# Conformer convolution: layout change of the product tiles by SBUF-to-SBUF transfers, and a provisional mean in half 0's layer norm

## The chip, the cores and the metric

The kernel runs on one core of a Trainium2 chip. The metric is the device time of one execution in microseconds (us). A change of under 0.2% (4.9 us) counts as no change here.

Five engines work side by side, each through its own list of instructions in order: TensorE (PE in the rows; PEld are its weight loads), VectorE (DVE), ScalarE (ACT), GpSimd (POOL) and SyncE (SP), which here only issues transfers. An instruction that waits holds up everything behind it in its engine's list. A transfer issued by ScalarE stands in ScalarE's list in the same way.

## The reference, cut to what matters

The program computes two layers over 1024 latent tokens with 1024 channels. The change is in the second layer's mixer, the Conformer convolution module:

```
u = xm @ w1 + b1;  a, g = split(u);  v = a * sigmoid(g)
v = depthwise conv along the tokens (31 taps) of v, + b
v = silu(layernorm(v))          # over the 1024 channels of a token
h = h + g1 * (v @ w2 + b2)
```

A feed-forward block and a final norm follow, which the change leaves alone.

## The kernel before

Channels lie on the 128 partitions and tokens on the free axis, so the 1024 channels are eight tiles m = 0 to 7, and the 1024 tokens are two halves of 512. Matrix products are made in three passes from a value split in a high and a low part (`whi`, `wlo` for weights, `xmh`, `xml` or `cxh`, `cxl` for data).

For each tile m, `conformer` does the following. TensorE makes the gate's product (`col_tile` into PSUM tile 0) and the value's (into tile 1). ScalarE takes the sigmoid into the tile `vt` (in the trace: `raw`), and VectorE multiplies in line 1253 or, in `taps`, line 1238. Then the depthwise convolution is made in one of two ways:

- Tiles 0, 2, 4 and 6 (`TAPS`): VectorE adds 30 shifted copies, one instruction each (line 1245, in the rows `CV<-ps,vec,CV`, some 1.3 us apart).
- Tiles 1, 3, 5 and 7 (`PRODS`): TensorE makes it as 108 small products (`conv`). For this the tile has to change its layout: tokens are grouped by their number modulo 4 (phases), and 32 channels times 4 phases must lie on the 128 partitions. The kernel writes the tile to DRAM (`vdr`) and reads it back rearranged into `xr` (also a `raw` buffer) with four transfers. ScalarE and VectorE split `xr` into `cxh` and `cxl`. After the products, VectorE copies PSUM tile 3 out to `yt` in two halves, and `yt` goes by way of DRAM (`cdr`) back to channel order in `yr` (in the rows: `sC`), from which ScalarE adds the bias into `CV`.

`conv(1)` follows tile 2's products, `conv(3)` those of tile 4, and `conv(5)` and `conv(7)` both follow tile 7's. Each needs five weight slots: four of eight steps, and a last one of four. Each slot is loaded by SyncE into one of two `wraw` buffers, copied to `whi` by ScalarE, and subtracted to `wlo` by GpSimd or VectorE in turns. A step is three products of 256 columns.

After that, half 0's layer norm (`center` with `sums`): the sum of the eight tiles is made from a running sum `lna[0]` (tiles 0 to 4) and the tiles 5, 6 and 7 (`LATE`) by products with an all-ones matrix; VectorE subtracts the mean from the eight tiles; ScalarE squares them; eight more products with ones give the variance; ScalarE takes the root and VectorE the reciprocal. Then the tiles are scaled, passed through silu, split (`xmh`, `xml`), and multiplied with w2 (`k_outer`).

The order of instructions on each engine is set by a planner in the program (`Order`): each operation has an estimated duration, a priority (`prio`, lower first) and buffers that it reads and writes, and the planner hands out the operation that it believes can start first. TensorE's order is the order in which the code calls it. A transfer costs SyncE `max(0.1, bytes / 340e3)` us in this plan and lands 2.0 us later; one on ScalarE costs 0.08 us. These are the plan's numbers, not the chip's. The program gives the transfers eight completion semaphores in turn: a transfer waits until the one that had its semaphore before has landed.

Of the kernel before, what the change touches and what calls it, by code (L numbers as in the profile page):

```python
# [21 lines left out]
ND = D // P  # L22
# [258 lines left out]
class Net:  # L281
    def __init__(self, nc, tc, es, a, out):
        self.nc, self.tc, self.a, self.out = nc, tc, a, out
        self.o = Order()
        self.mm_us = 0.2165
        pp = es.enter_context(tc.tile_pool(name="persist", bufs=1))
        ps = es.enter_context(tc.tile_pool(name="psum", bufs=1, space=bass.MemoryType.PSUM))
        dr = es.enter_context(tc.tile_pool(name="dram", bufs=1, space=bass.MemoryType.DRAM))
        self.P = [ps.tile([P, 2, 512], F32, name=f"ps{i}") for i in range(4)]
        self.PB = [[Buf(), Buf()] for _ in range(4)]  # L290
        self.vec = pp.tile([P, _NV], F32, name="vec")
        self.vB = Buf(True)
# [12 lines left out]
        self.ttall = pp.tile([P, 3 * 512], F32, name="tt")
        self.tt = Ring([(self.ttall[:, i * 512:i * 512 + 512], Buf()) for i in range(3)])
        self.acc = [(pp.tile([P, 512], F32, name=f"nacc{h}"), Buf()) for h in range(2)]
        self.rs = (pp.tile([P, 512], F32, name="rs"), Buf())
        self.mod = [pp.tile([P, 48], F32, name=f"mod{l}") for l in range(2)]
        self.modB = [[Buf() for _ in range(6)] for _ in range(2)]  # L310
        self.A = [pp.tile([P, 8], F32, name=f"A{n}") for n in range(5)]
        self.AB = [Buf(True) for _ in range(5)]
        self.gb = pp.tile([P, 8], F32, name="gb")
        self.gbB = Buf(True)
        self.eps = pp.tile([P, 1], F32, name="eps")
        self.epsB = Buf(True)
        self.sp8 = pp.tile([P, 2 * NR], F32, name="sp8")
        self.nsp8 = pp.tile([P, 2 * NR], F32, name="nsp8")
        self.nsp16 = pp.tile([P, 2 * NR], F32, name="nsp16")
        self.spB = Buf(True)  # L320
        self.cs = pp.tile([P, 16], F32, name="cs")
        self.modc = pp.tile([P, 16], F32, name="modc")
        self.cA = pp.tile([P, 8], F32, name="cA")
        self.ydr = dr.tile([NR, P, 1024], F32, name="ydr")
        self.ydrB = [[Buf(), Buf()] for _ in range(NR)]
        self.vdr = dr.tile([ND, P, 1024], F32, name="vdr")
        self.cdr = dr.tile([ND, P, 1024], F32, name="cdr")
        self.wq = []
        self.wq_load = self.wq_split = self.wq_use = 0
        self.wloaded, self.wsplit = {}, {}  # L330
# [862 lines left out]
    def conformer(self, pool):  # L1193
        nc, o = self.nc, self.o
        W, HS = 1024, 4
        CV = pool.tile([P, ND, W], F32, name="CV")
# [16 lines left out]
        phases = lambda t: t.rearrange("p (s i) -> p i s", i=4)  # L1213
        split = lambda t: t.rearrange("p (i s) -> p i s", i=4)
        flat = lambda pt: self.P[pt].rearrange("p a b -> p (a b)")
        inB = [Buf() for _ in range(ND)]
        outB = [[Buf(), Buf()] for _ in range(ND)]

        def sigmoid(m, pt):
            if m in TAPS:  # L1220
# [27 lines left out]
        def glu(m, pt):  # L1248

            if m in TAPS:  # L1250
                taps(m, pt)
                return
            self.stt(W, split(vt), phases(flat(pt)), self.v("cf_b_pw1", m), split(vt), ADD, MULT, self.PB[pt] + [vB], [vB], prio=-3)
            self.dma(self.vdr[m], vt, P * W * 4, r=[vB], w=[inB[m]], prio=-2)
            src = self.vdr[m].rearrange("(j c) (i s) -> i c j s", j=4, i=4)
            xrB.begin()
            for i in range(4):
                self.dma(split(xr)[32 * i:32 * i + 32], src[i], 131072, r=[inB[m]], wp=[xrB], prio=-2)
            hi, lo, hB, lB = xs[m // 2 % 2]
            inner = lambda t: t[:, :, HS:HS + 256]  # L1260
            self.act(W, inner(hi), split(xr), AF.Copy, [xrB], [hB], prio=-2)
            self.tten(W, inner(lo), split(xr), inner(hi).bitcast(F32), SUB, [xrB, hB], [lB], prio=-2)

        def conv(m):
            hi, lo, hB, lB = xs[m // 2 % 2]
            out = self.P[3].rearrange("p a (b s) -> p (a b) s", b=2)
            slot = None
            for j in range(4):
                for n, d in enumerate(SHIFTS):
                    i = j * len(SHIFTS) + n  # L1270
                    if i % 8 == 0:
                        slot = self.w_next()
                    wh, wl, whB, wlB = slot
                    c, s = slice(i % 8 * P, i % 8 * P + P), slice(HS + d, HS + d + 256)

                    def go():
                        for q, (w, x) in enumerate(((wh, hi), (wh, lo), (wl, hi))):
                            self.mm(out[:, j, :], w[:, c], x[:, j, s], n == 0 and q == 0, n == len(SHIFTS) - 1 and q == 2)

                    o.pe(3 * (256 / 2400 + 0.011), go, [whB, wlB, hB, lB], [self.PB[3][j // 2]])  # L1280
            for h in range(2):
                c = slice(512 * h, 512 * h + 512)
                self.ts(512, yt[:, c], self.P[3][:, h, :], 1.0, None, MULT, None, [self.PB[3][h]], [yB[h]], prio=-2)
                self.dma(self.cdr[m][:, c], yt[:, c], 262144, r=[yB[h]], w=[outB[m][h]], prio=-2)
            src = self.cdr[m].rearrange("(o c) (j s) -> j c o s", o=4, j=4)
            yrB.begin()
            for j in range(4):
                self.dma(split(yr)[32 * j:32 * j + 32], src[j], 131072, r=[outB[m][j // 2]], wp=[yrB], prio=-2)

            for h in range(2):  # L1290
                c = CV[:, m, h * 512:h * 512 + 512]
                self.act(
                    512, c.rearrange("p (s i) -> p s i", i=4), split(yr)[:, :, 128 * h:128 * h + 128].rearrange("p i s -> p s i"),
                    AF.Identity, [yrB], [cvB[m][h]], bias=self.v("cf_conv_b", m), prio=-1,
                )
            summed(m)

        for m in range(ND):
            if m == 0:
                self.first_pair()  # L1300
                sigmoid(m, 0)
            else:
                self.col_tile(self.w_next(), 0)
                sigmoid(m, 0)
                self.col_tile(self.w_next(), 1)
            glu(m, 1)
            hm = self.h[:, m, :]
            self.act(W, hm, hm, AF.Identity, self.hB[m] + [self.gbB], self.hB[m], bias=self.gb[:, m:m + 1], prio=2)
            for c in self.conv_after(m):
                conv(c)  # L1310
# [10 lines left out]
            for m in range(ND):  # L1321
                sums(m, *xs[m])

        var = self.P[1][:, 0, :]

        def sums(m, x, b):
            sq, sqB = self.tt.next()
            self.act(512, sq, x, AF.Square, [b], [sqB])
            o.pe(0.87, lambda: self.mm(var, self.ones, sq, m == 0, m == ND - 1), [self.onesB, sqB], [self.PB[1][0]])

        center(0, (0, 0), sums)
        self.rsqrt(512, rs2[0][0], var, [self.PB[1][0]], [rs2[0][1]])

        def deviation(bank):
            ms = self.stat(*lna[1], bank)
# [98 lines left out]
```

## Time and profile before

| | us |
|---|---|
| median of 3 runs | 2450.76 (2448.17 to 2450.9) |
| profiled execution, whole | 2447.42 |
| its span, first to last instruction | 2445.6 |
| TensorE busy | 2336.1 (96% of the span) |
| VectorE busy | 1915.0 (78%) |
| ScalarE busy | 966.6 (40%) |
| GpSimd busy | 808.0 (33%) |
| first product of the Conformer's `conv(1)` | starts at 1391.29 |
| first product with w2 | starts at 1591.50 |

The mean granted clock of TensorE is 0.98 of 2.4 GHz. Times in the rows are from the start of the span. In a timeline row stand start, length, engine, line and operation; in brackets the idle time of the engine just before it, and what ended it. Several instructions may be merged in one row (x8); the length then runs from the first's start to the last's end.

### The profile page before, as it was taken

The numbers are of one execution on the slowest core, as the hardware profiler recorded it, in microseconds if no ns is written. First come the engines' busy times: TensorE is split into PE (matmuls) and PEld (weight loads), VectorE is DVE, ScalarE is ACT, GpSimd is POOL, SyncE is SP. The second block draws the span as 40 slices with busy tenths as digits, with TensorE's granted clock in tenths as the row PEclk, the third lists the DMA queues.
The fourth block names the chain that finished last, engine by engine and source line by source line (L and its number), as shares of the span: only waits on it lengthen the run. The fifth ranks groups of instructions, "written<-read, shape, count | busy, mean of one in ns | idle before, by whom it ended". The sixth has DMA issues, their size and how long they took to land. (4 is left out here: it accounts for less than half of the span.)

```text
span 2445.6 us, 26204 instructions
## 1 busy us (share of the span) xinstructions
PE 2336.1 (96%) x10440; PEld 1893.9 (77%) x10440; DVE 1915.0 (78%) x1888; ACT 966.6 (40%) x1145; POOL 808.0 (33%) x413
## 2 busy tenths in 40 slices
PE   7999999889899999999998999699999999999997
PEld 2788788677688888888886888577788888888886
DVE  7677878776878778777888888677888777777877
ACT  5578778544433333333225332365322221222223
POOL 1100000355545554544423243245323322332323
PEclk9999999899999999999999999899999999999998
DMA  7324325352222323222111242422111111111101
GB/s 268 113 81 147 94 78 169 103 195 99 93 97 96 103 86 104 95 90 101 65 44 35 74 126 85 138 69 91 52 48 52 32 51 52 52 51 49 44 26 70
DMA packets 82443, 214.99 MB, mean 88 GB/s; under 512 B 8528, under 2 KB 33104, under 8 KB 82192
## 3 DMA queue, kind: packets, MB, share of 16 engines
q1 hardware_dynamic: 80448, 210.68, 26.4%
q10 hardware_dynamic: 1872, 2.62, 0.3%
q8 instruction: 82, 1.34, 0.2%
q14 instruction: 41, 0.34, 0.0%
HBM read 192.10 MB, written 13.63 MB: 84 GB/s over the span
## 5 line engine op out<-in xcount | busy, mean ns | idle before, releaser
L361 DVE SCALAR_TENSOR_TENSOR cv<-ps,vec,cv 128x960 f32<-128x960 f32 (+2 forms) x720 | 860.7, 1197 | 143.7 <-ACT cv L353 128.1
L440 PE MATMUL ps<-xmh,whi 128*128 128x512 f32 x2272 | 747.0, 396 | 19.3 <-ACT xmh L353 12.3
L440 PE MATMUL ps<-xmh,wlo 128*128 128x512 f32 x2272 | 739.9, 393 | 6.9 <-POOL wlo L368 5.2
L440 PE MATMUL ps<-xml,whi 128*128 128x512 f32 x2272 | 740.5, 393 | 4.2 <-DVE xml L361 4.1
L368 POOL TENSOR_TENSOR wlo<-wraw,whi 128x1024 fp32r<-128x1024 f32 (+1 forms) x164 | 397.8, 2440 | 703.0 <-ACT whi L353 689.4
L440 PEld LDWEIGHTS ps<-xmh,whi 128*128 128x128 f32 x2272 | 429.3, 190 | 117.7 <-ACT xmh L353 15.9
L440 PEld LDWEIGHTS ps<-xml,whi 128*128 128x128 f32 x2272 | 430.7, 190 | 102.9 <-DVE xml L361 8.4
L440 PEld LDWEIGHTS ps<-xmh,wlo 128*128 128x128 f32 x2272 | 430.2, 189 | 101.0 <-POOL wlo L368 7.8
L361 DVE SCALAR_TENSOR_TENSOR h<-ps,mod,h 128x512 f32<-128x512 f32 (+1 forms) x360 | 262.6, 733 | 161.6 <-PE ps L440 161.5
L353 ACT ACTIVATE cv<-ps,vec 128x1024 f32<-128x1024 f32 (+1 forms) x90 | 105.9, 1181 | 364.0 <-PE ps L440 352.9
L353 ACT ACTIVATE whi<-wraw 128x1024 fp32r<-128x1024 f32 (+1 forms) x198 | 202.2, 1042 | 111.0 <-DMA wraw<-w_out_in 34.1
L368 POOL TENSOR_TENSOR zl<-cv,zh 128x1024 fp32r<-128x1024 f32 x42 | 101.4, 2415 | 416.1 <-ACT zh L353 416.1
L440 PE MATMUL ps<-zh,dnh 128*128 128x512 f32 x576 | 227.8, 395 | 6.3 <-DVE h L361 5.9
L440 PE MATMUL ps<-zl,dnh 128*128 128x512 f32 x576 | 224.8, 390 | 5.0 <-POOL zl L368 5.0
L440 PE MATMUL ps<-zh,dnl 128*128 128x512 f32 x576 | 227.0, 394 | 0.0
L368 POOL TENSOR_TENSOR raw<-raw,sC 128x1024 f32<-128x1024 f32 x56 | 134.9, 2412 | 141.5 <-DMA raw<-ada_in 141.5
L353 ACT ACTIVATE cv<-cv 128x1024 f32<-128x1024 f32 (+1 forms) x46 | 47.1, 1023 | 309.3 <-DVE cv L361 301.0
L361 DVE SCALAR_TENSOR_TENSOR CV<-ps,vec,CV 128x1009 f32<-128x1009 f32 (+14 forms) x120 | 153.0, 1275 | 8.7 <-ACT CV L353 5.1
L368 POOL TENSOR_TENSOR dnl<-raw,dnh 128x512 fp32r<-128x512 f32 x72 | 93.5, 1299 | 176.6 <-ACT dnh L353 176.5
L353 ACT ACTIVATE raw<-raw 128x1024 f32<-128x1024 f32 x56 | 59.2, 1057 | 231.2 <-POOL raw L368 231.2
L440 PEld LDWEIGHTS ps<-zl,dnh 128*128 128x128 f32 x576 | 108.7, 189 | 31.2 <-POOL zl L368 5.8
L440 PEld LDWEIGHTS ps<-zh,dnh 128*128 128x128 f32 x576 | 108.4, 188 | 29.3 <-DVE h L361 6.4
(140 smaller groups left out, 2420.9 us busy)
## 6 DMA issues: line engine op xcount, KB each, us to landing
raw<-ada_in SPq DMA_DIRECT2D x88, 512.0 KB, 3.6
wraw<-up_in SPq DMA_DIRECT2D x88, 512.0 KB, 3.5
raw<-down_in SPq DMA_DIRECT2D x72, 256.0 KB, 3.1
wraw<-w_in SPq DMA_DIRECT2D x32, 512.0 KB, 3.4
wraw<-w_in_in SPq DMA_DIRECT2D x20, 512.0 KB, 3.4
wraw<-w_out_in SPq DMA_DIRECT2D x20, 512.0 KB, 3.6
wraw<-cw_in SPq DMA_DIRECT2D x16, 512.0 KB, 3.9
wraw<-gw_in SPq DMA_DIRECT2D x10, 512.0 KB, 3.9
```

The costliest lines, as they stand in the source:

```text
L353: "act", 0.2 + n * 0.00075, lambda: self.nc.scalar.activation(out, in_, func, **kw),
L361: lambda: self.nc.vector.scalar_tensor_tensor(out=out, in0=in0, scalar=scalar, in1=in1, op0=op0, op1=op1, **kw),
L368: return self.o.op(eng, dur, lambda: e.tensor_tensor(out=out, in0=in0, in1=in1, op=op), r, w, wp, prio=prio)
L440: self.nc.tensor.matmul(out, w, x, start=start, stop=stop)
```

## The change

The DRAM tiles `vdr` and `cdr` go. Each layout change is now 16 transfers of 32 partitions x 256 numbers (32 KB each) straight from SBUF to SBUF: 16 in place of one write and four reads on the way in, 16 in place of two writes and four reads on the way out. For tiles 1, 3 and 5 SyncE issues all of them; for tile 7 SyncE and ScalarE issue eight each, both on the way in and on the way out.

Half 0's layer norm no longer waits for the true mean. After the gate product of tile 7, `provisional` makes the mean of tiles 0 to 4 (one product with ones), ScalarE writes it scaled by 8/5 to `rs` (called `c`), and GpSimd subtracts it from these five tiles. VectorE subtracts `c` from tiles 5, 6 and 7 as they come. The squares are summed over all eight tiles around `c`; three products with ones sum the late tiles (`rest`, the difference between the true mean and `c`). The variance is the sum of squares less `rest` squared; then VectorE subtracts `rest` from the eight tiles.

```diff
+            for j in range(4):
+                for i in range(4):
+                    self.dma(split(xr)[32 * i:32 * i + 32, j, :], split(vt)[32 * j:32 * j + 32, i, :], 32768,
+                        r=[vB], wp=[xrB], prio=-2, eng=("sp", "act")[i % 2 if m == ND - 1 else 0])
-            self.dma(self.vdr[m], vt, P * W * 4, r=[vB], w=[inB[m]], prio=-2)
-            for i in range(4):
-                self.dma(split(xr)[32 * i:32 * i + 32], src[i], 131072, r=[inB[m]], wp=[xrB], prio=-2)
...
+            mu, muB = self.P[3][:, 0, :], self.PB[3][0]
+            o.pe(0.87, lambda: self.mm(mu, self.ones, lna[0][0], True, True), [self.onesB, lna[0][1]], [muB])
+            self.act(512, c, mu, AF.Copy, [muB], [cB], scale=ND / (ND - len(LATE)))
+                if m not in LATE:
+                    self.tten(512, x, x, c, SUB, [b, cB], [b], eng="pool", prio=1)
...
+            if m in LATE:
+                self.tten(512, x, x, c, SUB, [b, cB], [b], prio=-3)
+            self.act(512, sq, x, AF.Square, [b], [sqB], prio=-1)
+            o.pe(0.87, lambda: self.mm(var, self.ones, sq, m == 0, m == ND - 1), [self.onesB, sqB], [varB])
+            if m in LATE:
+                o.pe(0.87, lambda: self.mm(rest, self.ones, x, m == LATE[0], m == LATE[-1]), [self.onesB, b], [restB])
+        self.act(512, dd, rest, AF.Square, [restB], [ddB])
+        self.tten(512, c, var, dd, SUB, [varB, ddB, cB], [cB], prio=-3)
+        self.rsqrt(512, c, c, [cB], [cB])
+            self.tten(512, x, x, rest, SUB, [b, restB], [b], prio=-1)
-        center(0, (0, 0), sums)
-        self.rsqrt(512, rs2[0][0], var, [self.PB[1][0]], [rs2[0][1]])
```

The way out of `conv` is changed in the same manner as the way in. The planner, with its estimates unchanged, also hands out some other instructions in another order. Three places follow; `ps_66`, `ps_67` and `ps_68` are the PSUM tiles 1, 2 and 3, and `raw_76` and `raw_77` are `vt` and `xr`.

On VectorE, from tile 1's gated product to tile 2's, before:

```order
L361 SCALAR_TENSOR_TENSOR raw_76<-ps_66,vec,raw_76 128x1024
L361 SCALAR_TENSOR_TENSOR CV<-ps_67,vec,CV 128x1022
L361 SCALAR_TENSOR_TENSOR CV<-ps_67,vec,CV 128x1021
L361 SCALAR_TENSOR_TENSOR CV<-ps_67,vec,CV 128x1020
L361 SCALAR_TENSOR_TENSOR CV<-ps_67,vec,CV 128x1019
L361 SCALAR_TENSOR_TENSOR CV<-ps_67,vec,CV 128x1018
L361 SCALAR_TENSOR_TENSOR CV<-ps_67,vec,CV 128x1017
L361 SCALAR_TENSOR_TENSOR CV<-ps_67,vec,CV 128x1016
L361 SCALAR_TENSOR_TENSOR CV<-ps_67,vec,CV 128x1015
L368 TENSOR_TENSOR cxl_7831<-raw_77,cxh_7830 128x4x256
L368 TENSOR_TENSOR wlo_83<-wraw_79,whi_82 128x1024
```

and of the change:

```order
L359 SCALAR_TENSOR_TENSOR raw_76<-ps_66,vec,raw_76 128x1024
L359 SCALAR_TENSOR_TENSOR CV<-ps_67,vec,CV 128x1022
L359 SCALAR_TENSOR_TENSOR CV<-ps_67,vec,CV 128x1021
L359 SCALAR_TENSOR_TENSOR CV<-ps_67,vec,CV 128x1020
L359 SCALAR_TENSOR_TENSOR CV<-ps_67,vec,CV 128x1019
L359 SCALAR_TENSOR_TENSOR CV<-ps_67,vec,CV 128x1018
L366 TENSOR_TENSOR cxl_7829<-raw_77,cxh_7828 128x4x256
L359 SCALAR_TENSOR_TENSOR CV<-ps_67,vec,CV 128x1017
L359 SCALAR_TENSOR_TENSOR CV<-ps_67,vec,CV 128x1016
L366 TENSOR_TENSOR wlo_83<-wraw_79,whi_82 128x1024
L359 SCALAR_TENSOR_TENSOR CV<-ps_67,vec,CV 128x1015
```

The low part of tile 1's rearranged data, `cxl`, moved three taps forward: five taps of tile 0 stand between it and the gated product, where there were eight.

On SyncE, from the third weight slot of `conv(7)` to the first transfers of its result, before:

```order
L342 DMA wraw_79<-cw_in 128x1024
L342 DMA cdr<-yt 128x512 x2
L342 DMA wraw_78<-cw_in 128x1024
L342 DMA sC<-cdr 32x4x256 x4
L342 DMA wraw_79<-cw_in 128x512
L342 DMA wraw_78<-w_in 128x1024
L342 DMA wraw_79<-w_in 128x1024
L342 DMA cdr<-yt 128x512 x2
```

and of the change:

```order
L340 DMA wraw_79<-cw_in 128x1024
L340 DMA sC<-yt 32x256 x16
L340 DMA wraw_78<-cw_in 128x1024
L340 DMA wraw_79<-cw_in 128x512
L340 DMA wraw_78<-w_in 128x1024
L340 DMA wraw_79<-w_in 128x1024
L340 DMA sC<-yt 32x256 x8
```

The load of the fourth weight slot (`wraw_78<-cw_in`) stood behind two writes of `conv(5)`'s result; it stands behind all sixteen of its transfers now.

On VectorE, from the copy of `conv(7)`'s result to the reciprocal, before:

```order
L376 TENSOR_SCALAR yt<-ps_68 128x512 x2
L368 TENSOR_TENSOR CV<-CV,ps_65 128x512 x8
L383 RECIPROCAL rs<-rs 128x512
L368 TENSOR_TENSOR CV<-CV,rs 128x512 x4
L368 TENSOR_TENSOR xml_75<-CV,xmh_73 128x512
```

and of the change:

```order
L374 TENSOR_SCALAR yt<-ps_68 128x512 x2
L366 TENSOR_TENSOR CV<-CV,rs 128x512 x3
L366 TENSOR_TENSOR CV<-CV,ps_67 128x512 x2
L366 TENSOR_TENSOR rs<-ps_66,tt 128x512
L366 TENSOR_TENSOR CV<-CV,ps_67 128x512 x6
L381 RECIPROCAL rs<-rs 128x512
L366 TENSOR_TENSOR CV<-CV,rs 128x512 x4
```

Eight subtractions stood before the sum of squares; now eight that need `rest` stand behind it, all of them ahead of the reciprocal, two even ahead of the variance (`rs<-ps_66,tt`).

## Rows read from the trace of the kernel before

**Rows 1.** Waits of TensorE from 1340 to 1600: total, times, longest.

```profile
PE ps L440 <- ACT CV L353: 9.3, 1, 9.3
...
PE ps L440 <- DVE yt L376: 3.8, 2, 3.0
```

**Rows 2.** Timeline of TensorE, conv(7)'s last product to the first with w2.

```profile
1560.31 0.28 PE L440 MATMUL ps<-cxh,wlo 128*128 128x256 f32 x1
...
1572.51 2.08 PE L440 MATMUL ps<-CV,ones 128*128 128x512 f32 x2 [9.34 <-ACT CV L353]
1576.02 8.77 PE L440 MATMUL ps<-tt,ones 128*128 128x512 f32 x16 [1.44 <-ACT tt L353]
1591.50 0.79 PE L440 MATMUL ps<-xmh,whi 128*128 128x512 f32 x1 [6.71 <-ACT xmh L353]
```

**Rows 3.** Timeline of SyncE's transfers, tile 1's way in.

```profile
1372.35 0.33 SPq L342 DMA_DIRECT2D vdr<-raw  x1
1374.97 1.75 SPq L342 DMA_DIRECT2D raw<-vdr  x4
```

**Rows 4.** Timeline of ScalarE, the copy behind tile 1's way in.

```profile
1379.46 1.06 ACT L353 ACTIVATE cxh<-raw 128x1024 fp32r<-128x1024 f32 x1 [17.44 <-DMA raw<-vdr]
```

**Rows 5.** Timeline of VectorE, tile 1's gated product to tile 2's.

```profile
1371.05 1.28 DVE L361 SCALAR_TENSOR_TENSOR raw<-ps,vec,raw 128x1024 f32<-128x1024 f32 x1
1372.24 10.47 DVE L361 SCALAR_TENSOR_TENSOR CV<-ps,vec,CV 128x1022 f32<-128x1022 f32 x8
1382.62 1.22 DVE L368 TENSOR_TENSOR cxl<-raw,cxh 128x1024 fp32r<-128x1024 f32 x1
...
1395.03 1.29 DVE L361 SCALAR_TENSOR_TENSOR ps<-ps,vec,raw 128x1024 f32<-128x1024 f32 x1
...
1398.79 1.22 DVE L368 TENSOR_TENSOR wlo<-wraw,whi 128x1024 fp32r<-128x1024 f32 x1
```

**Rows 6.** Tile sd, filled from SBUF by 32 to 64 rows: issue ns min/median/max, landing us.

```profile
L342 SPq DMA_DIRECT2D sd<-uh x24: 507/556/1669, 100.3 to 412.7; - x24
...
DMA to landing us min/median/max: 2.4/3.2/8.2
```

**Rows 7.** Timeline of TensorE, the 75th product of conv(1).

```profile
1400.10 0.34 PE L440 MATMUL ps<-cxh,wlo 128*128 128x256 f32 x1
```

**Rows 8.** Waits of VectorE from 1340 to 1600.

```profile
DVE ps L361 <- PE ps L440: 7.7, 1, 7.7
```

**Rows 9.** Timeline of VectorE around conv(5)'s end and conv(7)'s fourth weight slot.

```profile
1529.50 1.28 DVE L361 SCALAR_TENSOR_TENSOR raw<-ps,vec,raw 128x1024 f32<-128x1024 f32 x1
...
1543.11 0.68 DVE L376 TENSOR_SCALAR yt<-ps 128x512 f32<-128x512 f32 x1
...
1554.52 1.22 DVE L368 TENSOR_TENSOR wlo<-wraw,whi 128x1024 fp32r<-128x1024 f32 x1
```

**Rows 10.** Timeline of SyncE's transfers, conv(5)'s way out and conv(7)'s fourth weight slot.

```profile
1544.99 1.11 SPq L342 DMA_DIRECT2D cdr<-yt  x2
1546.90 0.33 SPq L342 DMA_DIRECT2D wraw<-cw_in  x1
```

**Rows 11.** Page, transfers: count, KB each, us to landing.

```profile
wraw<-cw_in SPq DMA_DIRECT2D x16, 512.0 KB, 3.9
```

**Rows 12.** Timeline of ScalarE, the bias copies of conv(5)'s and conv(7)'s results.

```profile
1554.81 2.38 ACT L353 ACTIVATE CV<-sC,vec 128x512 f32<-128x512 f32 x2 [1.47 <-DMA sC<-cdr]
...
1571.29 2.24 ACT L353 ACTIVATE CV<-sC,vec 128x512 f32<-128x512 f32 x2 [7.67 <-DMA sC<-cdr]
```

**Rows 13.** Windows: busy us of each engine, granted clock, DMA share, GB/s.

```profile
1540.00:1550.00 10.00, 5.97 (x36) 5.40 (x36) 8.66 (x9) 3.79 (x4) 2.38 (x2) 0.83 0.54 171
1590.00:1600.00 10.00, 8.39 (x19) 5.08 (x20) 5.80 (x10) 6.76 (x10) 0.00 (x0) 0.68 0.00 0
```

**Rows 14.** Timeline of VectorE, half 0's norm.

```profile
1574.62 4.87 DVE L368 TENSOR_TENSOR CV<-CV,ps 128x512 f32<-128x512 f32 x8 [12.71 <-PE ps L440]
1585.86 3.35 DVE L383 RECIPROCAL rs<-rs 128x512 f32<-128x512 f32 x1 [6.37 <-ACT rs L353]
```

More of the change, by code (lines that the diff above doesn't have):

```diff
@@ L325, in __init__ @@
         self.ydrB = [[Buf(), Buf()] for _ in range(NR)]
-        self.vdr = dr.tile([ND, P, 1024], F32, name="vdr")
-        self.cdr = dr.tile([ND, P, 1024], F32, name="cdr")
         self.wq = []
@@ L1215, in conformer @@
         flat = lambda pt: self.P[pt].rearrange("p a b -> p (a b)")
-        inB = [Buf() for _ in range(ND)]
-        outB = [[Buf(), Buf()] for _ in range(ND)]
         def sigmoid(m, pt):
@@ L1253, in glu @@
             self.stt(W, split(vt), phases(flat(pt)), self.v("cf_b_pw1", m), split(vt), ADD, MULT, self.PB[pt] + [vB], [vB], prio=-3)
-            self.dma(self.vdr[m], vt, P * W * 4, r=[vB], w=[inB[m]], prio=-2)
-            src = self.vdr[m].rearrange("(j c) (i s) -> i c j s", j=4, i=4)
             xrB.begin()
-            for i in range(4):
-                self.dma(split(xr)[32 * i:32 * i + 32], src[i], 131072, r=[inB[m]], wp=[xrB], prio=-2)
+            for j in range(4):
+                for i in range(4):
+                    self.dma(
+                        split(xr)[32 * i:32 * i + 32, j, :], split(vt)[32 * j:32 * j + 32, i, :], 32768,
+                        r=[vB], wp=[xrB], prio=-2, eng=("sp", "act")[i % 2 if m == ND - 1 else 0],
+                    )
             hi, lo, hB, lB = xs[m // 2 % 2]
@@ L1283, in conv @@
                 self.ts(512, yt[:, c], self.P[3][:, h, :], 1.0, None, MULT, None, [self.PB[3][h]], [yB[h]], prio=-2)
-                self.dma(self.cdr[m][:, c], yt[:, c], 262144, r=[yB[h]], w=[outB[m][h]], prio=-2)
-            src = self.cdr[m].rearrange("(o c) (j s) -> j c o s", o=4, j=4)
             yrB.begin()
             for j in range(4):
-                self.dma(split(yr)[32 * j:32 * j + 32], src[j], 131072, r=[outB[m][j // 2]], wp=[yrB], prio=-2)
+                for o_ in range(4):
+                    self.dma(
+                        split(yr)[32 * j:32 * j + 32, o_, :], split(yt)[32 * o_:32 * o_ + 32, j, :], 32768,
+                        r=[yB[j // 2]], wp=[yrB], prio=-2, eng=("sp", "act")[o_ % 2 if m == ND - 1 else 0],
+                    )
             for h in range(2):
@@ L1296, in conv, with half0, provisional @@
             summed(m)
+        def half0(m):
+            return CV[:, m, :512], cvB[m][0]
+        def provisional():
+            c, cB = rs2[0]
+            mu, muB = self.P[3][:, 0, :], self.PB[3][0]
+            o.pe(0.87, lambda: self.mm(mu, self.ones, lna[0][0], True, True), [self.onesB, lna[0][1]], [muB])
+            self.act(512, c, mu, AF.Copy, [muB], [cB], scale=ND / (ND - len(LATE)))
+            for m in range(ND):
+                if m not in LATE:
+                    x, b = half0(m)
+                    self.tten(512, x, x, c, SUB, [b, cB], [b], eng="pool", prio=1)
         for m in range(ND):
@@ L1304, in conformer @@
                 sigmoid(m, 0)
+                if m == ND - 1:
+                    provisional()
                 self.col_tile(self.w_next(), 1)
@@ L1322, in center @@
                 sums(m, *xs[m])
-        var = self.P[1][:, 0, :]
-        def sums(m, x, b):
-            sq, sqB = self.tt.next()
-            self.act(512, sq, x, AF.Square, [b], [sqB])
-            o.pe(0.87, lambda: self.mm(var, self.ones, sq, m == 0, m == ND - 1), [self.onesB, sqB], [self.PB[1][0]])
-        center(0, (0, 0), sums)
-        self.rsqrt(512, rs2[0][0], var, [self.PB[1][0]], [rs2[0][1]])
+        var, varB = self.P[1][:, 0, :], self.PB[1][0]
+        rest, restB = self.P[2][:, 0, :], self.PB[2][0]
+        c, cB = rs2[0]
+        for m in range(ND):
+            x, b = half0(m)
+            if m in LATE:
+                self.tten(512, x, x, c, SUB, [b, cB], [b], prio=-3)
+            sq, sqB = self.tt.next()
+            self.act(512, sq, x, AF.Square, [b], [sqB], prio=-1)
+            o.pe(0.87, lambda: self.mm(var, self.ones, sq, m == 0, m == ND - 1), [self.onesB, sqB], [varB])
+            if m in LATE:
+                o.pe(0.87, lambda: self.mm(rest, self.ones, x, m == LATE[0], m == LATE[-1]), [self.onesB, b], [restB])
+        dd, ddB = self.tt.next()
+        self.act(512, dd, rest, AF.Square, [restB], [ddB])
+        self.tten(512, c, var, dd, SUB, [varB, ddB, cB], [cB], prio=-3)
+        self.rsqrt(512, c, c, [cB], [cB])
+        for m in range(ND):
+            x, b = half0(m)
+            self.tten(512, x, x, rest, SUB, [b, restB], [b], prio=-1)
         def deviation(bank):
```

## The prediction

> **What bounds the kernel now.** The page comes first: TensorE is busy for 96% of the span, so a change counts only where it moves a wait of TensorE. The list of TensorE's waits over the Conformer's stretch [rows 1] shows what lies at its end: 9.3 us for the bias copy of tile 7's convolution, and 3.8 us for `conv(5)`'s copy to `yt`. The timelines give the places. `conv(7)`'s last product starts at 1560.31, so it is done near E = 1560.4; the first product with w2 starts at 1591.5, after a wait of 6.7 for the first split tile [rows 2]. In these 31.1 us TensorE makes 12 small products with ones and else stands. The change aims there. But TensorE is not free before that: in `conv(1)` and `conv(7)` its weight slots arrive just as it wants them, and there I expect the loss.
>
> **Part 1, the way in of tile 1.** Before, SyncE writes tile 1 at 1372.35 and issues four reads in 1.75 us [rows 3]; ScalarE's copy starts at 1379.46 [rows 4]. VectorE comes to `cxl` only at 1382.62, after eight taps, and waits for nothing [rows 5]. Now `cxl` stands behind five taps, which at 10.47 / 8 = 1.31 each end at 1378.8. The 16 transfers start at the same 1372.35. No row shows one of 32 x 256 numbers between SBUF tiles. The nearest for the issue are 0.33 for a single one [rows 3] and 0.507 at least, 0.556 mostly, for rows from SBUF to SBUF [rows 6]; the four reads went out (1.75 - 0.33) / 3 = 0.47 apart. I take 0.5 apart, between the last two, with the ends 0.33 and 0.6. For the landing I take 2.4, the least of [rows 6], since 32 KB is less than any of those; ends 2.0 and 3.2. Then the last one is issued at 1372.35 + 15 x 0.5 = 1379.85 and lands at 1382.25; the copy takes 1.06 [rows 4], so `cxl` starts at 1383.3 and VectorE has stood 4.5 us. It can't give them back: its list runs without a gap from there to tile 2's gated product at 1395.03. Behind that stands a `wlo` at 1398.79, done at 1400.01 [rows 5], and TensorE takes up that very slot in `conv(1)` at 1400.10 [rows 7]. So all of TensorE's work from there on comes 4.5 us later. The ends give 1372.35 + 5.0 + 2.0 + 1.06 - 1378.8 = 1.6, and with 9.0 + 3.2 in place of 5.0 + 2.0 it is 6.8.
>
> The ways in of tiles 3 and 5 cost nothing: the same delay, some 3 us in the landing, ends where VectorE waits for TensorE anyway, up to 7.7 us at a time [rows 8]. Without this cover each could cost what tile 1 costs.
>
> **Part 2, tile 7: `conv(5)` and `conv(7)`.** (Times on the old clock, without part 1.) The product for the provisional mean takes TensorE about 0.9, and VectorE has one more tap ahead of the gated product, which therefore starts not at 1529.5 but at 1530.8 [rows 9] and ends at 1532.1. Its transfers go out on two engines, eight each: four in 2.0, the fifth when the first has landed, at 2.4, the last at 1532.1 + 2.4 + 1.5 = 1536.0, to land at 1538.4. ScalarE has these eight ahead of its copy of `conv(5)`'s fourth slot, which so ends near 1537.6. Behind it VectorE makes that slot's `wlo`, a tap, `cxl`, and four taps (one before), and comes to `yt` near 1546.2 in place of 1543.11 [rows 9].
>
> Then SyncE. The load for `conv(7)`'s fourth slot went out at 1546.90, behind two writes [rows 10]. Now 16 transfers stand before it, from `yt`'s first half at 1546.8 on: it goes out at 1554.8 and lands within 3.9 [rows 11], by 1558.7. ScalarE has the two bias copies of `conv(5)`'s result ahead of that slot's copy: the last transfer lands at 1554.3 + 2.4 = 1556.7, the two copies take 2.4 [rows 12], to 1559.1, the weight copy 1.06, `wlo` 1.22: done at 1561.4. Before, it was done at 1554.52 + 1.22 = 1555.74 [rows 9], and TensorE took it up at once. So E comes 5.7 us later. With the ends: 1546.8 + 5.0 + 2.0 + 2.4 + 2.3 = 1558.5, that is 2.8 late; 9.0 and 3.2 give 1563.7, 8.0 late.
>
> Both stalls may also cost clock: around the 3.0 us wait for `yt` the granted clock of that window was 0.83, which over 5.97 busy us makes 1.0 [rows 13]. I add 0.5 for the two together, with ends 0 and 2.
>
> **Part 3, the norm.** From E to tile 7's bias copy at 1571.29 [rows 12] it was 10.9 us. Now: 0.9 for `yt`'s first half, then on ScalarE 2.4 and 2.0 for its eight issues, a square (0.6), a weight copy (1.06) and a square, 7.6, by when the last transfer has landed (0.9 + 2.4 + 1.5 + 2.4 = 7.2). That wins 3.3. From the bias copy to the last sum, before, 1584.8 - 1571.3 = 13.5. Now two bias copies (2.2), a square, and nine products with ones, six for the squares and three for `rest`; eight took 8.77, partly at the low clock [rows 2], so nine take 9.9, in all 12.7: 0.8 won. From the last sum to the reciprocal, before, 1585.86 - 1584.8 = 1.1. Now two subtractions (4.87 / 8 = 0.61 each [rows 14]), the variance (0.7), and six more subtractions that VectorE has ahead of the reciprocal (3.7) and that hide the root: 5.7, so 4.6 lost. In all 0.5 lost, between 3 won (faster landing, sums at full clock) and 3.5 lost. GpSimd's five subtractions lie where it waits for ScalarE's weight copies and cost nothing; if they held up a `wlo` of `conv(5)`, 1 to 2 us.
>
> **The sum.** 4.5 + 5.7 + 0.5 + 0.5 = 11.2 us. Behind it TensorE is the bound, with few waits that could give it back. The profiled execution took 2447.42 (its span and 1.8 around it), so 2458.6 on its scale; it lay 3.3 below the median of the runs shown, 2450.76, and on that scale the time is 2462. The lower ends add up to 1.6 + 2.8 - 3 = +1.4, the upper to 6.8 + 8.0 + 2 + 3.5 = +20.3.
>
> **The rivals.**
>
> *Faster: the data are there before their readers.* If the transfers go out so fast that `cxl` finds its data, parts 1 and 2 vanish, the tail wins its 3, and TensorE begins w2 at the full clock (8.39 busy us at 0.68 cost 2.7 [rows 13]): 2450.8 - 5.7 = 2445. For it speaks the wait of 7.67 for the way out [rows 12], which goes with the trip by DRAM. It decides from 16 issues and a landing within 1377.7 - 1372.35 = 5.4 us on, that is 0.22 apart, and no issue in [rows 3, 6] is under 0.3.
>
> *No change: the lower ends hold.* 1.6 + 2.8 + 0.5 = 4.9: 2455; or one of the two delays has a cover that I don't see, which leaves 5 to 6.
>
> *Much slower: the small transfers don't overlap.* If each holds its place until others have landed and they go out 1.0 apart (some of [rows 6] were issued for 1.669), part 1 is 12.0 and part 2 is 13.7 late: 2477. It decides from 0.75 apart on. Against it: the four reads went out 0.47 apart and their data were used 4.5 us after the first issue [rows 3, 4], so what is fixed in a landing overlaps and only the issue adds up.
>
> The Trainium skill (DMA: Bandwidth & Descriptors, section Rules for kernel authors) says that many small transfers should be merged into one large one, as below 64 KB one pays mostly overhead. That speaks against the whole change, and taken one after another it is this last rival. The trace agrees in part: the overhead adds up in the issuing engine's list, not in the landings.
>
> **How the numbers follow.** A difference under 0.2%, 4.9 us, can't be told from none. Chances: the forecast (5 to 16 us slower) 0.6, much slower 0.12, no change 0.2, faster 0.08. So slower by over 0.2% has 0.72, within 0.2% has 0.2, faster 0.08. The likeliest case's own range is 2456 to 2467. The range for 8 in 10 reaches into the no-change case, down to 2450, and up to the upper ends, 2470.
>
> **What would show it.** In the changed profile: VectorE idle for 2 to 7 us ahead of tile 1's `cxl`, released by ScalarE's `cxh`; TensorE waiting for a `wlo` in `conv(1)` and again at `conv(7)`'s fourth slot; SyncE's sixteen issues of `conv(5)`'s way out spread over 7 to 9 us, and the weight load behind them; the reciprocal 5 to 6 us after the last sum; the first w2 product some 11 us later than 1591.5. The prediction is wrong if issues follow each other in under 0.35, if VectorE finds its data at `cxl`, or if from E to w2 it takes well under 31 us.

## The result, and the profile after

The changed kernel takes 2463.1 us (median of 6 runs, 2457.99 to 2468.7), the kernel before 2449.47 (6 runs, 2447.39 to 2451.08). The ratio is 1.0066, with an interval of 1.0055 to 1.0076: slower, where 2462 and slower were forecast. The two profiled executions lie further apart than the medians, 2465.24 and 2447.42. Of these 17.8 us, 1.35 arose before the Conformer, in the first 700 us, where both run the same instructions.

This table is made from the starts of TensorE's products in the two traces:

| start of | before | after | later by |
|---|---|---|---|
| first product of `conv(1)` | 1391.29 | 1392.64 | 1.35 |
| first product of `conv(3)` | 1449.69 | 1454.84 | 5.15 |
| first product of `conv(5)` | 1527.89 | 1533.94 | 6.05 |
| first product of `conv(7)` | 1543.94 | 1555.89 | 11.95 |
| last product of `conv(7)` | 1560.31 | 1578.37 | 18.06 |
| first product with w2 | 1591.50 | 1609.96 | 18.46 |

So 3.8 us were lost from `conv(1)` to `conv(3)`, 0.9 from there to `conv(5)`, 5.9 in `conv(5)`, 6.1 in `conv(7)`, and 0.4 in the tail. Behind w2 0.7 came back.

The waits of TensorE after, from 1340 to 1620 (in all, times, longest). They answer to [rows 1]; the columns are the same:

```profile
PE ps L438 <- ACT xmh L351: 11.8, 1, 11.8
PE ps L438 <- ACT whi L351: 8.3, 3, 3.2
PE ps L438 <- ACT tt L351: 7.4, 2, 7.0
PE ps L438 <- DVE yt L374: 2.9, 2, 2.1
PE ps L438 <- DVE wlo L366: 2.5, 3, 1.0
```

The weight slots, `whi` and `wlo`, are new at the top: 10.8 us in three places. The 9.3 for tile 7's bias copy are gone, and two waits in the norm stand in their place (7.0 for the squares `tt`, 11.8 instead of 6.7 for the first split tile).

Where those three places are shows in TensorE's timeline after (start, length, in brackets the idle time and its releaser):

```profile
1403.67 0.39 PE L438 MATMUL ps<-cxh,whi 128*128 128x256 f32 x1 [2.29 <-ACT whi L351]
...
1405.16 0.39 PE L438 MATMUL ps<-cxh,wlo 128*128 128x256 f32 x1 [0.98 <-DVE wlo L366]
...
1545.48 0.39 PE L438 MATMUL ps<-cxh,whi 128*128 128x256 f32 x1 [2.80 <-ACT whi L351]
...
1547.33 0.41 PE L438 MATMUL ps<-cxl,whi 128*128 128x256 f32 x1
1547.55 0.41 PE L438 MATMUL ps<-cxh,wlo 128*128 128x256 f32 x1
...
1571.57 0.38 PE L438 MATMUL ps<-cxh,whi 128*128 128x256 f32 x1 [3.20 <-ACT whi L351]
...
1578.37 0.28 PE L438 MATMUL ps<-cxh,wlo 128*128 128x256 f32 x1
...
1609.96 0.79 PE L438 MATMUL ps<-xmh,whi 128*128 128x512 f32 x1 [11.81 <-ACT xmh L351]
```

They are the fourth slots of `conv(1)`, `conv(5)` and `conv(7)`. After each of these stalls, and after `conv(7)`'s waits for `yt`, there is a stretch of products that start 0.21 apart (1547.33, 1547.55), where 0.12 is usual: the lower of the two clock levels (1.2 and 2.4 GHz). In `conv(1)` it runs from 1406.24 to 1409.63.

The transfers, in SyncE's timeline after (SPq and ACTq are the transfers in the lists of SyncE and ScalarE), and the issue and landing of tile 1's (issue ns min/median/max; landing in us):

```profile
1373.71 10.01 SPq L340 DMA_DIRECT2D raw<-raw  x16
...
1538.04 5.86 SPq L340 DMA_DIRECT2D raw<-raw  x8
...
1555.77 10.02 SPq L340 DMA_DIRECT2D sC<-yt  x16
1565.89 1.01 SPq L340 DMA_DIRECT2D wraw<-cw_in  x2
```

```profile
L340 SPq DMA_DIRECT2D raw<-raw x16: 517/589/592, 1373.7 to 1383.1; - x16
...
DMA to landing us min/median/max: 1.8/1.8/1.9
```

Sixteen issues take 10.0 us: (1383.1 - 1373.7) / 15 = 0.63 apart. `conv(7)`'s fourth weight load stands behind sixteen of them and goes out at 1565.89, before it was 1546.90 [rows 10].

What VectorE and ScalarE did, after:

```profile
1373.59 6.54 DVE L359 SCALAR_TENSOR_TENSOR CV<-ps,vec,CV 128x1022 f32<-128x1022 f32 x5
1386.12 1.23 DVE L366 TENSOR_TENSOR cxl<-raw,cxh 128x1024 fp32r<-128x1024 f32 x1 [5.99 <-ACT cxh L351]
...
1400.14 1.29 DVE L359 SCALAR_TENSOR_TENSOR ps<-ps,vec,raw 128x1024 f32<-128x1024 f32 x1
...
1571.55 1.23 DVE L366 TENSOR_TENSOR wlo<-wraw,whi 128x1024 fp32r<-128x1024 f32 x1 [5.49 <-ACT whi L351]
...
1600.74 3.67 DVE L366 TENSOR_TENSOR CV<-CV,ps 128x512 f32<-128x512 f32 x6
1604.32 3.35 DVE L381 RECIPROCAL rs<-rs 128x512 f32<-128x512 f32 x1
```

```profile
1401.47 1.21 ACT L351 ACTIVATE CV<-ps,vec 128x1024 f32<-128x1024 f32 x1 [0.21 <-DVE ps L359]
1402.57 1.56 ACT L351 ACTIVATE whi<-wraw 128x1024 fp32r<-128x1024 f32 x2
...
1538.04 6.21 ACTq L339 DMA_DIRECT2D raw<-raw  x8
1544.37 1.06 ACT L351 ACTIVATE whi<-wraw 128x1024 fp32r<-128x1024 f32 x1 [17.42 <-DMA raw<-raw]
...
1567.24 2.28 ACT L351 ACTIVATE CV<-sC,vec 128x512 f32<-128x512 f32 x2 [8.53 <-DMA sC<-yt]
1570.47 1.58 ACT L351 ACTIVATE whi<-wraw 128x1024 fp32r<-128x1024 f32 x2 [0.95 <-DMA wraw<-cw_in]
...
1579.46 5.50 ACTq L339 DMA_DIRECT2D sC<-yt  x8
1585.01 0.63 ACT L351 ACTIVATE tt<-CV 128x512 f32<-128x512 f32 x1 [7.85 <-DMA sC<-yt]
...
1587.01 2.27 ACT L351 ACTIVATE CV<-sC,vec 128x512 f32<-128x512 f32 x2
```

`cxl` stands 5.99 us after five taps, as the order said. Twice a weight copy of ScalarE follows eight or sixteen transfers directly: at 1544.37 behind its own eight issues, at 1570.47 behind the load that SyncE sent so late.

The windows (busy us of PE, PEld, DVE, ACT, POOL with counts, granted clock, DMA share, GB/s), first before, then after:

```profile
1400.00:1420.00 20.00, 18.62 (x98) 15.62 (x97) 19.54 (x18) 5.59 (x6) 8.37 (x4) 1.00 0.62 184
1540.00:1560.00 20.00, 15.71 (x113) 14.73 (x113) 15.47 (x14) 8.69 (x9) 6.05 (x3) 0.91 0.54 165
```

```profile
1400.00:1420.00 20.00, 16.53 (x87) 14.22 (x86) 18.28 (x17) 7.00 (x8) 9.22 (x4) 0.91 0.29 92
1540.00:1560.00 20.00, 13.56 (x75) 12.75 (x74) 14.14 (x13) 5.92 (x6) 4.89 (x3) 0.74 0.41 122
1560.00:1580.00 20.00, 14.69 (x94) 14.06 (x93) 9.65 (x10) 4.92 (x5) 5.31 (x3) 0.84 0.36 111
```

The clock's share, busy time by what is missing to 1: after, 13.56 x 0.26 + 14.69 x 0.16 = 5.9 us in `conv(5)` and `conv(7)`, before 15.71 x 0.09 = 1.4. In `conv(1)` it is 16.53 x 0.09 = 1.5 after and nothing before.

### The profile page after: what moved, and what is told of

It reads as the page before. It is cut to its first block, busy times and chain, and to the rows that moved or that the text cites. A ratio compares the mean times of both kernels' runs of the same rounds, so it can differ in the third digit from the quotient of the medians.

```text
span 2463.4 us, 26334 instructions
## 1 busy us (share of the span) xinstructions
PE 2347.2 (95%) x10440; PEld 1903.1 (77%) x10440; DVE 1916.3 (78%) x1892; ACT 967.1 (39%) x1147; POOL 812.5 (33%) x418
```

## The experiments

Three theories were set against each other first. Q: the sixteen small transfers issue one after the other, and what stands behind them or waits for them sets TensorE back. N: the new norm does it. O: the order that the planner makes from a wrong price for the transfers does it. All kernels are compared with the kernel before on the same chip; the five columns are times between starts of products in each kernel's profile, as in the table above.

| kernel | ratio (interval) | conv(1) to (3) | (3) to (5) | (5) to (7) | (7) to its last | to w2 |
|---|---|---|---|---|---|---|
| before | 1 | 58.4 | 78.2 | 16.1 | 16.4 | 31.2 |
| after | 1.0066 (1.0055-1.0076) | 62.2 | 79.1 | 22.0 | 22.5 | 31.6 |
| e1 | 1.0061 (1.0049-1.0073) | 63.8 | 78.2 | 21.8 | 22.8 | 29.5 |
| e2 | 0.9991 (0.9983-1.0000) | 58.6 | 79.4 | 16.3 | 16.2 | 31.1 |
| e3 | 1.0055 (1.0043-1.0067) | 56.4 | 79.1 | 20.5 | 26.1 | 31.8 |
| e4 | 0.9998 (0.9990-1.0007) | 58.4 | 79.1 | 16.6 | 16.3 | 31.0 |
| e5 | 1.0042 (1.0026-1.0057) | 56.4 | 79.1 | 21.6 | 22.1 | 31.1 |
| e6 | 1.0062 (1.0049-1.0076) | 63.7 | 79.1 | 16.1 | 23.5 | 33.4 |
| e7 | 1.0042 (1.0029-1.0056) | 62.2 | 79.1 | 21.9 | 16.6 | 31.1 |
| e8 | 0.9965 (0.9952-0.9977) | 56.4 | 79.1 | 16.3 | 16.1 | 22.6 |
| e9 | 1.0058 (1.0045-1.0072) | 59.1 | 79.1 | 21.4 | 23.1 | 31.6 |
| e10 | 1.0116 (1.0102-1.0130) | 67.8 | 79.1 | 21.6 | 23.4 | 31.5 |
| e11 | 0.9971 (0.9961-0.9981) | 58.5 | 79.1 | 16.5 | 16.5 | 26.0 |
| e12 | 0.9952 (0.9938-0.9966) | 56.4 | 79.1 | 14.2 | 15.4 | 23.0 |

The column for `conv(1)` to `conv(3)` also holds up to 2.2 us that none of these edits sets; the last section tells what they are.

**e1, the transfers alone.** The changed kernel with the old norm:

```diff
-                if m == ND - 1:
-                    provisional()
...
+        center(0, (0, 0), sums)
+        self.rsqrt(512, rs2[0][0], var, [self.PB[1][0]], [rs2[0][1]])
```

> The SBUF-to-SBUF transfers with the old layer norm of half 0. Theory Q (the serial issue of the small transfers, 0.63 us each in the profile of the changed kernel, and what is queued behind them make the loss): conv(1) +3.8, conv(5) and conv(7) +11 (no product for the provisional mean), the tail -3.3 for the faster way out: 2461. Rival N (the new norm makes the loss: its product, GpSimd's subtractions and the late reciprocal): 2446, since only the gain of the way out is left. In the profile Q wants VectorE to stand 5 to 6 us ahead of tile 1's cxl again.

Measured: 2462.81, ratio 1.0061. Q holds, N falls: without the new norm the loss stays whole. The product for the provisional mean shows too: from `conv(3)` to `conv(5)` it is 78.2 as before, and 79.1 or more wherever the product is made.

**e2, the norm alone.** The other half: `vdr` and `cdr` as before, the new norm.

> The new norm of half 0 with all layout changes by way of DRAM as before. Theory Q: 0.9 for the product, 0.8 won in the sums, 4.6 lost as six subtractions stand ahead of the reciprocal: 2454. Rival N: the whole loss, 2463 or more.

Measured: 2445.14, ratio 0.9991. N falls again. Q's price of 5 us for the norm was too high: `conv(7)`'s end to w2 takes 31.1 as before, since the sums end sooner (18.7 us behind `conv(7)`'s last product, before 23.9) by as much as the six subtractions cost. Whether the norm alone gains 2 us or nothing isn't settled; its interval touches 1.

**e3, the planner with the measured price.**

```diff
-        return self.o.op("sp", max(0.1, nbytes / 340e3), lambda: e.dma_start(out=out, in_=in_), r, w, wp, after=after, lat=2.0, prio=prio)
+        return self.o.op("sp", 0.63 if nbytes == 32768 else max(0.1, nbytes / 340e3), lambda: e.dma_start(out=out, in_=in_), r, w, wp, after=after, lat=1.2200000000000002 if nbytes == 32768 else 2.0, prio=prio)
```

The latency is 1.85 less the 0.63; ScalarE's transfers get the same two numbers (0.08 and 2.3 before).

> The changed kernel, but the planner takes 0.63 us of the engine for each 32 KB transfer and 1.85 to its landing (0.1 or 0.08, and 2.1 to 2.4 before), as its profile shows them. It then puts tile 1's cxl behind ten taps, not five. Theory Q: only conv(1)'s 3.8 come back, tile 7's transfers still stand ahead of the weight copy and the weight load: 2459. Rival O (the loss is the order that the planner made by a wrong price, the transfers themselves can be hidden): 2449 or less.

Measured: 2460.02, ratio 1.0055, so O falls. Tile 1's loss is indeed gone (56.4 from `conv(1)` to `conv(3)`), as VectorE has ten taps to do before `cxl`. But tile 7 has no such work to put in front: SyncE's sixteen issues of `conv(5)`'s way out still stand ahead of the weight load, and ScalarE's bias copies, which wait for the last of them, ahead of the weight copies. TensorE in e3:

```profile
1537.01 0.39 PE L438 MATMUL ps<-cxh,whi 128*128 128x256 f32 x1 [2.45 <-ACT whi L351]
...
1561.25 0.58 PE L438 MATMUL ps<-cxh,whi 128*128 128x256 f32 x1 [7.92 <-ACT whi L351]
```

The wait at `conv(7)` grew from 3.2 to 7.9 us: what tile 1 gave back, tile 7 took in part.

**e4, only the last way out.** The new norm, and `conv(7)`'s way out alone from SBUF to SBUF.

> The new norm, and from SBUF to SBUF only the way out of conv(7), on both queues; all other layout changes by way of DRAM. Theory Q: 0.9 for the product, -3.3 for the way out, -0.8 and +4.6 in the norm: 2451. Rival N: 2460 or more. Against the norm alone it prices the way out by itself: Q says 3.3 us less.

Measured: 2445.97, ratio 0.9998. N falls, but the way out doesn't win its 3.3 us either: from `conv(7)`'s end to w2 it is 31.0, against 31.1 in e2, although the bias copy comes 2.8 us earlier (8.4 and 11.2 behind the last product). ScalarE in e4 shows why:

```profile
1561.92 5.25 ACTq L341 DMA_DIRECT2D sC<-yt  x8
1567.21 0.63 ACT L353 ACTIVATE tt<-CV 128x512 f32<-128x512 f32 x1 [7.63 <-DMA sC<-yt]
```

Its eight issues hold the engine for 5.25 us, and the squares of the early tiles, which were ready, stand behind them. So the sums begin late and end 18.6 us behind `conv(7)`'s last product, as in e2. That is tested in e8.

**e5 to e7, one transfer undone at a time.** Each is the changed kernel with one way sent by DRAM again:

```diff
+            if m not in (3, 5, 7):     # e5: tile 1's way in; e6: (1, 3, 5); e7: conv(5)'s way out, m not in (1, 3, 7)
+                self.dma(self.vdr[m], vt, P * W * 4, ...)
+                ... four reads as before
```

> The changed kernel with one transfer undone: tile 1's way in goes by way of DRAM again. Theory Q (serial issues): conv(1) starts no later weight slot, 3.8 to 5.4 us come back, 2458.5; all else as in the changed kernel. Rival H (the delay of tile 1 is made good later, since conv(7) waits anyway): 2463, the same as the changed kernel.

> The changed kernel with one transfer undone: tile 7's way in goes by way of DRAM again, so ScalarE has no eight issues ahead of conv(5)'s fourth weight copy. Theory Q: conv(5) stands no longer at its fourth slot and keeps its clock, 6 us come back, 2457. Rival L (only the weight load behind conv(5)'s way out sets conv(7)'s end, the stall in conv(5) moves into it): 2461 or more.

> The changed kernel with one transfer undone: conv(5)'s way out goes by way of DRAM again, so that two writes and not sixteen transfers stand ahead of conv(7)'s fourth weight load. Theory Q: conv(7) stands no longer at its fourth slot, 6 us come back, 2457. Rival L': the slot waits for tile 7's late yt anyway, 2461 or more.

Measured: e5 2456.35 and e7 2456.59 (each 1.0042), e6 2462.01 (1.0062). Beside 1.0066, tile 1's way in and `conv(5)`'s way out are worth some 6 us each (Q: 3.8 to 5.4, and 6); in their profiles just the one stretch is short again (56.4; 16.6). In e6 Q's 6 us did not come: in time its rival L was right. `conv(5)` is short again (16.1, so 5.9 won), but little of it reaches the end. TensorE in e6:

```profile
1548.95 0.36 PE L440 MATMUL ps<-cxh,whi 128*128 128x256 f32 x1 [3.07 <-DVE yt L376]
...
1564.97 0.58 PE L440 MATMUL ps<-cxh,whi 128*128 128x256 f32 x1 [4.63 <-ACT whi L353]
```

The stall at `conv(7)`'s slot is still there and 1.4 us longer, as L has it, but that takes back only 1.0 us of the 5.9 (23.5 for 22.5). In this profile 1.8 more went in the tail, where the products with ones ran at the lower clock (33.4 to w2), and 1.5 from `conv(1)` to `conv(3)`, which the edit doesn't touch. So L's mechanism is shown for a part only, and what the stall of `conv(5)` is worth by itself stays open.

**e8, the tail in another order.** As e4, and:

```diff
-            self.act(512, sq, x, AF.Square, [b], [sqB], prio=-1)
+            if 1 <= m <= 6:
+                self.tten(512, sq, x, x, MULT, [b], [sqB], prio=-1)
+            else:
+                self.act(512, sq, x, AF.Square, [b], [sqB], prio=-3)
...
-            self.tten(512, x, x, rest, SUB, [b, restB], [b], prio=-1)
+            self.tten(512, x, x, rest, SUB, [b, restB], [b], prio=1)
```

> As e4 (only the way out of conv(7) from SBUF to SBUF), with the tail put in another order: the squares of tiles 1 to 6 are made by VectorE, so that they don't stand behind ScalarE's eight issues, and the six subtractions of the rest don't stand ahead of the reciprocal. Theory P (in e4 ScalarE's eight issues, 5.25 us, held up the squares and so the nine sums, and the six subtractions held up the reciprocal): from conv(7)'s end to the first product with w2 25 us in place of 31.0, so 2441. Rival C (the sums are bound by TensorE at its low clock, and the chain from bias copy to reciprocal): 30 us and 2446.

Measured: 2437.74, ratio 0.9965 (0.9952 to 0.9977): faster than both kernels, and more than P had asked. VectorE in e8:

```profile
1560.72 2.59 DVE L368 TENSOR_TENSOR tt<-CV 128x512 f32<-128x512 f32 x4
...
1574.92 1.27 DVE L368 TENSOR_TENSOR CV<-CV,ps 128x512 f32<-128x512 f32 x2
1576.11 3.35 DVE L383 RECIPROCAL rs<-rs 128x512 f32<-128x512 f32 x1
```

Four squares are made while the transfers still go out, two subtractions in place of six stand ahead of the reciprocal, and w2 begins 22.6 us behind `conv(7)`'s last product. The reciprocal starts 8.5 us earlier than in e4, 16.9 instead of 25.4 behind that product: 6.0 of it because the sums end at 12.7 and not at 18.6, and 2.5 for the subtractions. The two edits were made together, so this division is read from the profiles and was not tried apart. The 2.0 us less from `conv(1)` to `conv(3)` (56.4 for e4's 58.4) are not e8's edit.

**e9, tile 1 on two queues, and e10, twice as many transfers.**

```diff
-   eng=("sp", "act")[i % 2 if m == ND - 1 else 0]
+   eng=("sp", "act")[i % 2 if m in (1, ND - 1) else 0]              # e9
...
+   for c in ((slice(0, 128), slice(128, 256)) if m == 1 else (slice(0, 256),)):   # e10: one transfer for each
```

> The changed kernel, with tile 1's sixteen transfers shared by SyncE and ScalarE, eight each, as tile 7's are. Theory Q (each queue issues one after the other): the last lands about 7.5 us after the first issue, as tile 7's did, not 11.3; VectorE stands 3.5 us ahead of cxl (four taps before it) in place of 6.0, and conv(1) gets 2.5 us back: 2460.5. Rival R (what limits lies behind the queues and is shared): the stall stays at 6 or more, 2463.

> The changed kernel, with each of tile 1's sixteen transfers cut into two of half the width: 32 of 16 KB, the same bytes. Theory Q (the price is one of the count): 32 x 0.63 = 20.2 us of issues, VectorE stands 14.8 us ahead of cxl (six taps before it), 2472. Rival B (the price is one of the bytes): 10.1 us of issues, a stall of about 5, 2462.

Measured: e9 2460.93 (1.0058), e10 2475.44 (1.0116). Both as Q says. VectorE in e9 and in e10, and SyncE in e10:

```profile
1381.13 1.23 DVE L366 TENSOR_TENSOR cxl<-raw,cxh 128x1024 fp32r<-128x1024 f32 x1 [2.68 <-ACT cxh L351]
```

```profile
1397.10 1.23 DVE L366 TENSOR_TENSOR cxl<-raw,cxh 128x1024 fp32r<-128x1024 f32 x1 [15.45 <-ACT cxh L351]
```

```profile
1373.91 20.86 SPq L340 DMA_DIRECT2D raw<-raw  x32
```

With two queues VectorE's stall falls from 5.99 to 2.68; with twice the count at the same bytes it rises to 15.45, and 32 issues take 20.86 us, 0.65 each. In e10 TensorE also waits 4.1 us for `cxh` ahead of `conv(1)`, which the columns leave out. The price is one of the count and of the queue. In time, e9's interval overlaps that of the changed kernel, so its gain rests on the stall and on 59.1 in place of 62.2. The Trainium skill (DMA: Bandwidth & Descriptors, section Issuing engines are not separate DMA queues) says that a second issuing engine saves only the time to initiate a transfer, usually small beside the transfer. Here that time was no small part: 9.4 of the 11.3 us from the first issue to the last landing.

**e11, the same tail with no transfer from SBUF to SBUF.**

> As e8, but conv(7)'s way out goes by way of DRAM too, so that no layout change is left from SBUF to SBUF: the new norm with the tail's order of e8. It prices conv(7)'s way out by itself in a tail in which nothing else waits. Theory W: the bias copy comes 2.8 us later (11.2 and 8.4 us behind conv(7)'s end in e2 and e4), and so does all behind it: 2440.5, E to w2 25.4. Rival V (the way out is hidden again, behind the sums): 2437.7 as e8, 22.6.

Measured: 2439.57, ratio 0.9971 (0.9961 to 0.9981). In the profile W holds: w2 begins 26.0 us behind `conv(7)`'s last product, 3.4 later than in e8. The ratios of e8 and e11 overlap, so in time the way out's gain isn't shown. Most of e8's gain is the tail's order.

**e12, `conv(7)` in another PSUM tile.**

```diff
-            out = self.P[3].rearrange("p a (b s) -> p (a b) s", b=2)
+            pt = 0 if m == ND - 1 else 3
+            out = self.P[pt].rearrange("p a (b s) -> p (a b) s", b=2)
```

> As e8, and conv(7) adds up in another PSUM tile (0, which tile 7's sigmoid has left) than conv(5), so that its first product needn't wait for VectorE's copy of conv(5)'s result to yt; no order changes. Theory Y: TensorE's two waits for yt, 3.2 + 0.8 us, and half a microsecond to one of clock go: 2433. Rival Z (conv(7)'s weight slots are only just in time, so the wait moves to a slot): 2436 to 2438.

Measured: 2434.72, ratio 0.9952 (0.9938 to 0.9966), the best of all. Theory Y holds in the profile: no wait for `yt` is left in TensorE's list, and from `conv(5)` to `conv(7)` it is 14.2 in place of 16.3. A part came back as a new wait, 2.1 us for tile 7's `cxh` and `cxl`. Its interval overlaps with e8's, so against e8 the gain in time is likely, not shown.

## Why the prediction was right, step by step

**The way in of tile 1: right in place, and near in size by some luck.** Forecast was a stall of 4.5 us ahead of `cxl` (1.6 to 6.8), measured 5.99. The issues go 0.63 apart, not 0.5; the landing takes 1.85, not 2.4. Both lie outside the ends that I gave them (0.33 to 0.6, and 2.0 to 3.2), on opposite sides.

"It can't give them back" did not hold. VectorE makes a `wlo` behind `cxl`, and it took 1.22 us where it had taken 3.42. Before, with GpSimd's `wlo` beside it:

```profile
1383.76 3.42 DVE L368 TENSOR_TENSOR wlo<-wraw,whi 128x1024 fp32r<-128x1024 f32 x1
1383.49 2.61 POOL L368 TENSOR_TENSOR wlo<-wraw,whi 128x1024 fp32r<-128x1024 f32 x1 [20.02 <-ACT whi L353]
```

and after:

```profile
1389.77 1.22 DVE L366 TENSOR_TENSOR wlo<-wraw,whi 128x1024 fp32r<-128x1024 f32 x1
1390.09 3.16 POOL L366 TENSOR_TENSOR wlo<-wraw,whi 128x1024 fp32r<-128x1024 f32 x1 [25.26 <-ACT whi L351]
```

So 2.2 of the 5.99 came back: tile 2's gated product starts 1400.14 - 1395.03 - 1.35 = 3.8 later, and TensorE lost 3.8 too. Against e5, where VectorE's `wlo` took 1.22 as well, it is 5.8. That 4.5 lies between the two is luck.

The way there was a little different: the first wait is for a `whi`, because ScalarE's weight copy (1402.57) stands behind the first tap of tile 2 (1401.47), which waits for VectorE's gated product (1400.14); the `wlo` follows. The clock's 1.5 us in `conv(1)`, for which I had no term, lie within the 3.8.

That the ways in of tiles 3 and 5 cost nothing held. Tile 3's lies between `conv(1)` and `conv(3)`, which take 56.4 with it (e5) and without it (e8). Tile 5's lies between `conv(3)` and `conv(5)`, 79.1 with and without it.

**Tile 7: right in place, wrong in one size.** The two places are as forecast: eight issues of ScalarE ahead of `conv(5)`'s fourth weight copy (e6), and sixteen of SyncE ahead of `conv(7)`'s fourth load (e7). Forecast were 5.7 us of delay and 0.5 for the clock. Measured, from `conv(5)`'s start to `conv(7)`'s last product, are 12.0. The waits make 6.6 of it: 3.6 and 4.0 at the two slots, less 0.9 that the wait for `yt` got shorter. The rest, 5.4, is clock. The windows give 4.5; counted product by product, what each start takes beyond 0.119 adds up to 6.9 after and 1.3 before, so 5.5. So the term that was mis-sized is the clock: "I add 0.5 for the two together, with ends 0 and 2". It was read from one stall of 3.0 us; here there are six waits in three places, with 5.8, 5.6 and 3.4 us of products 0.21 apart behind them. What I also missed is that `conv(5)`'s fourth slot makes TensorE itself stand: I had the weight copy end near 1537.6. TensorE wanted that slot at 1536.46 before, or near 1537.4 with the 0.9 of the new product, and ScalarE's eight issues took 6.2 us and not the 3.9 that I had.

**The product for the provisional mean** had no term of its own in the sum; it cost 0.9, as the times from `conv(3)` to `conv(5)` show.

**The tail: right in sum, its parts less so.** Forecast +0.5, measured 0.4: the bias copy 2.3 us sooner (forecast 3.3), the sums 2.4 shorter (0.8), from the last sum to the reciprocal 5.1 longer (4.6). e8 shows that the sums were held back by ScalarE's own issues, which I had counted only against the bias copy. The bias copy itself comes 8.4 us behind `conv(7)`'s last product in e8, as in e4.

**The rivals.** *Much slower* needed issues 0.75 apart; they were 0.63. *Faster* needed 0.22. *No change* fell with both delays.

**The sum.** Without the 1.35 from before the Conformer, the profiled pair differs by 16.4, where 11.2 were forecast: 3.8 for 4.5, 0.9 for none, 6.6 for 5.7, 5.4 for 0.5, 0.4 for 0.5, and 0.7 won behind w2. The medians differ by 13.6 only, and the forecast started from a median of 2450.76 that six runs put at 2449.47; so that 2462 lies so near to 2463.1 is luck: a clock ten times too small, hidden by the difference between the profiled pair and the medians.

## What to carry to other kernels

Price a transfer by its place in the list of the engine that issues it. Sixteen small ones were ten microseconds of that list here, and the cost fell on the next weight load or weight copy behind them, two engines away. And look at what a faster transfer's own issues hold up: the tail won 8 us only in e8, when the squares no longer stood behind ScalarE's eight issues and six subtractions no longer ahead of the reciprocal.

## What the runs showed of the hardware that was not expected

- A 32 x 256 transfer between SBUF tiles keeps the issuing queue for 0.59 us (0.63 from one to the next), against 0.43 for the four reads from DRAM with four times the bytes; half the bytes cost the same (0.65 in e10).
- With both queues at work for tile 7's way in, sixteen issues still took 6.2 us, not 5.0, and the first landed after 3.1 to 3.3 us, not 1.85. In e9, for tile 1's, the same took 5.3, and no landing over 2.1. What makes the difference was not tried.
- Two profiles of the same instructions can differ by 2 us from `conv(1)` to `conv(3)`: 58.4 in e4, 56.4 in e8, whose lists agree there. The traces show where it comes from. Behind tile 1's `cxl` VectorE and GpSimd each make a `wlo` at nearly the same time, and the one that starts second takes longer. Where GpSimd starts first, by 0.04 to 0.3 us, VectorE's takes 3.4 (before, e2, e4, e11: 58.4 to 58.6). Where VectorE starts first, its own takes 1.2 and GpSimd's up to 3.45, against 2.4 alone (e5, e8, e12: 56.4). With tile 1's way in from SBUF to SBUF it is 2.8 in e1 and e6 (63.8 and 63.7), and 1.2 in the changed kernel and e7 (62.2). In e4, as before, TensorE then waits 1.3 us for a `wlo` of GpSimd behind `conv(1)`; in e8 it doesn't. What decides who starts first was not tried. VectorE and GpSimd in e8:

```profile
1383.70 1.22 DVE L368 TENSOR_TENSOR wlo<-wraw,whi 128x1024 fp32r<-128x1024 f32 x1
1384.53 2.67 POOL L368 TENSOR_TENSOR wlo<-wraw,whi 128x1024 fp32r<-128x1024 f32 x1 [21.08 <-ACT whi L353]
```
